# HGRN scores with the queries stationary: four 32-query blocks in four column quarters, one masked copy, a transpose back

## The chip, the cores and the metric

The kernel runs on one core of one Trainium2 chip. The metric is device time in microseconds of one execution of the whole block, median over runs.

## The reference, cut to what matters

A decoder block: 16 meta tokens and 1024 tokens of width 1024 go through an S5 branch and an HGRN2 branch, which are merged, projected and followed by a gated MLP. The change touches the intra-chunk part of the HGRN2 branch, for 8 heads of 128 channels:

```python
def hgrn2_mixer(q, f_logit, i_in, og, lb, norm_g):
    ...
    cum = jnp.cumsum(heads(log_f), axis=3)
    q_in = qh * jnp.exp(cum)
    k_in = kh * jnp.exp(-cum)
    ...
    def chunk_step(state, xs):
        qi, ki, ko, v, dec = xs
        scores = jnp.where(causal, jnp.einsum('bhtd,bhsd->bhts', qi, ki), 0.0)
        o = jnp.einsum('bhts,bhsv->bhtv', scores, v) + jnp.einsum('bhtd,bhdv->bhtv', qi, state)
        state = dec[..., None] * state + jnp.einsum('bhsd,bhsv->bhdv', ko, v)
        return state, o
```

All data are float32.

## The kernel before

The work runs in three stretches. First the projections of the input (`proj_tile`, L166: weights `wh`, `wl` stationary, 24 matmuls of 342 columns to a tile `pj`). From about 195 us to 880 us the loop over heads `h` follows: `main_steps` projects head `h` and some gates (`ga`), one tile per step, while the generators in `fill` advance head `h - 1` (`hgrn_mix`, two halves of 512 tokens) and two S5 halves (`s5_half`); the tables `MIX0`, `MIX1`, `S5A`, `S5B` say at which step each generator is advanced. In the last round (`h` = 8) there is no head left to project, only gates. Then come the output projections, beginning with `whgrn` (`bh`, `bl_`, L935 and after), and the MLP.

The program is not executed in the order written: a scheduler puts the instructions of each engine into a fixed order at build time, and the pools `pj` (3 banks of PSUM), `sm` (5 banks) and the SBUF tags limit how far it may run ahead. On the chip each engine, and SP's DMA queue, works through its own list in that order.

A half of `hgrn_mix` handles 4 chunks of 128 tokens. Each chunk's scores are made in 4 blocks of 32 queries, each against all the keys up to the end of the block: with the keys `Kb` stationary (32, 64, 96 or 128 columns) and 32 queries of `Qb` moving (L726), so scores land with keys on the partitions. Four masked copies, one for each 32 partitions (`copy_predicated`, L734), put them into `sT`, whose never written entries are zero. One step later `sT` is the stationary operand of the output matmuls (L742), next to the state term (L743); `o_norm`, a transpose back (L628) and a gating (`gt`) follow. After the second half `yb_d[h]` is written to DRAM (L748). A float32 matmul shows as two passes in the trace, each a weight load and a matmul; a transpose shows as one.

After the last head, SP loads `mc` from `ga_d` and `yr` from `yb_d` (L932, L934), ACT casts `yr` into `bh`, and the `whgrn` projections begin.

Of the kernel before, what the change touches and what calls it, by code (L numbers as in the profile page):

```python
# [15 lines left out]
ALU = mybir.AluOpType  # L16
# [4 lines left out]
P = 128  # L21
# [30 lines left out]
def block_kernel(  # L52
# [5 lines left out]
    V, S, G, PE, SY = nc.vector, nc.scalar, nc.gpsimd, nc.tensor, nc.sync  # L58
# [19 lines left out]
    def bc(ap, ax, shape):  # L78
        return ap.unsqueeze(ax).to_broadcast(shape)
# [6 lines left out]
    def cst(shape, name, dt=F32):  # L86
        return const.tile(shape, dt, name=name)
# [4 lines left out]
    def sm():  # L92
        return psums[-1].tile([P, 512], F32, tag="sm", name="sm", bufs=1 if len(psums) == 1 else 5)
# [3 lines left out]
    ident = cst([P, P], "ident")  # L97
# [104 lines left out]
    cmask = s5c.tile([P, P], U8, name="cmask")  # L202
# [10 lines left out]
    def masks():  # L213
        for m, starts in ((mV, [(0, 32)]), (mC, []), (mE, [(31, 32)])):
            G.memset(m, 0.0)
            for a, st in starts:
                G.memset(m[:, 0:512].rearrange("p (a b) -> p a b", b=st)[:, :, a : a + 1], 1.0)
        G.memset(mV[:, 512:513], 1.0)
        G.memset(mV[:, 16:528].rearrange("p (a b) -> p a b", b=128)[:, :, 0:1], 1.0)
        G.memset(mC[:, 0:1], 1.0)  # L220
        G.memset(mC[:, 16:528].rearrange("p (a b) -> p a b", b=128)[:, :, 0:1], 1.0)
        G.memset(mE[:, 16:528].rearrange("p (a b) -> p a b", b=128)[:, :, 127:128], 1.0)
        G.memset(mE[:, 15:16], 1.0)
        cmf = p1.tile([P, P], F32, name="cmf")
        G.memset(cmf, 1.0)
        for r in range(4):
            R = slice(32 * r, 32 * r + 32)
            G.affine_select(
                out=cmf[R, 0:32], in_=cmf[R, 0:32], pattern=[[1, 32]], compare_op=ALU.is_ge, fill=0.0, base=0,
                channel_multiplier=-1,  # L230
            )
        V.tensor_copy(out=cmask, in_=cmf)

    def small_consts():
# [245 lines left out]

    consts = small_consts()
    masks()
    for k in range(NK):
        for i, (raw, hi, lo) in enumerate(w01):
# [10 lines left out]
    for k in range(NK):  # L495
# [5 lines left out]
        for s, l in x_cols(k):  # L501
            e = slice(s, s + l)
# [73 lines left out]
    def half(name):  # L576
        return hps[1].tile([P, HB], F32, tag="hh", name=name, bufs=NHH)
# [30 lines left out]
    def chunks(ap):  # L608
        return ap.rearrange("p (n b) -> p n b", n=4)
# [24 lines left out]
    def hgrn_mix(h, hh, carry, q, f, vT, gt):  # L634
        if True:
# [16 lines left out]
            W4 = Wp[:, 16:528].rearrange("p (a b) -> p a b", b=32)  # L652
            Rt, Qb, ko = half("R"), half("Qb"), half("ko")
            R4 = Rt[:, 0:512].rearrange("p (a b) -> p a b", b=32)
# [11 lines left out]
            for i in (1, 2, 3):  # L666
                w = 32 * i - 16
# [37 lines left out]
            for n in range(nn):  # L705
                PE.matmul(  # L706
                    pp[:, n * P : (n + 1) * P], kot[:, n * P : (n + 1) * P], vtok[:, n * P : (n + 1) * P], start=True,
                    stop=True,
# [12 lines left out]
            psc = sm()  # L721
            for n in range(4):
                for i in range(4):
                    e = 16 + KN * n + 128 * i
                    m = 32 * (i + 1)
                    PE.matmul(  # L726
                        psc[:m, n * P + 32 * i : n * P + 32 * i + 32], Kb[:, e : e + m],
                        Qb[:, n * P + 32 * i : n * P + 32 * i + 32], start=True, stop=True,
                    )
            sT = sTs[hh]  # L730
            for r in range(4):
                R = slice(32 * r, 32 * r + 32)
                w = P - 32 * r
                V.copy_predicated(  # L734
                    out=sT[R, :, 32 * r : P], mask=bc(cmask[R, 0:w], 1, [32, 4, w]),
                    data=psc[R, :].rearrange("p (n b) -> p n b", n=4)[:, :, 32 * r : P],
                )
            yield
            po = sm()
            for n in range(4):  # L740
# [9 lines left out]
    def s5_half(hb):  # L750
# [107 lines left out]
        out=m16, in_=m16, pattern=[[1, 2]], compare_op=ALU.is_ge, fill=0.0, base=T0, channel_multiplier=-1  # L858
# [18 lines left out]
            yield from hgrn_proj_in(h, st)  # L877
        yield from gate_steps(NGATE[h])

    MIX0 = {0: 1, 1: 1, 2: 1, 3: 1, 5: 1, 6: 1}  # L880
    MIX1 = {4: 1, 5: 1, 7: 1, 8: 1, 10: 1, 11: 1}
    S5A = {0: 1, 2: 1, 3: 1, 4: 1, 5: 1, 6: 1}
    S5B = {8: 1, 9: 1, 10: 1, 11: 1, 12: 1, 13: 1}
    prev = []
# [13 lines left out]
    Kb = hp.tile([P, 16 + 4 * KN], F32, name="Kb")  # L898
    sTs = [hp.tile([P, 4, P], F32, name=f"sT{i}") for i in range(2)]
    KTs = [sp.tile([P, 4, P], F32, name=f"KT{i}") for i in range(1)]  # L900
    for t in sTs + KTs:
        G.memset(t, 0.0)
    for h in range(1, NK + 1):
        st = []
        carry = hp.tile([P, P], F32, tag="carry", name="carry", bufs=2)
        fill = [
            (hgrn_mix(h - 1, 0, carry, *prev), MIX0), (hgrn_mix(h - 1, 1, carry, *prev), MIX1),
            (s5_half(2 * h - 2), S5A), (s5_half(2 * h - 1), S5B),
        ]
        for u, _ in enumerate(main_steps(h, st)):  # L910
            for g, when in fill:
                step(g, when.get(u, 0))
        for g, _ in fill:
            step(g, 99)
        prev = st
# [74 lines left out]
    for m in range(NK):  # L990
# [15 lines left out]
        for a in range(2):  # L1006
            pt_ = sm()
            for i in range(4):
# [3 lines left out]
                out=ht[:, 4 * a : 4 * a + 4, m * P : (m + 1) * P], in_=pt_.rearrange("p (n b) -> p n b", n=4)  # L1012
# [190 lines left out]
```

## Time and profile before

| | |
|---|---|
| median of 3 runs | 2039.78 us (2030.02 to 2045.96) |
| profiled execution: its own time | 2034.58 us |
| span of its trace | 2032.9 us |
| PE busy | 1982.1 us (98%) |
| DVE busy | 1259.6 us (62%) |
| ACT busy | 563.9 us (28%) |
| mean granted TensorE clock | 0.982 of full speed |

PE is the matmul engine, PEld its weight loads, DVE the vector engine, ACT the scalar engine, SPq the queue from which SP issues DMAs. Since matmuls are pipelined, the recorded durations of neighbours overlap: what a matmul costs is the distance from its start to the next one's. [...]

### The profile page before, as it was taken

To read this page: it belongs to the slowest core of one execution; us is meant where nothing else is said; L and a number is where in the kernel's file an instruction comes from. 1 tells how busy PE (TensorE), PEld (TensorE's weight loads), DVE (VectorE), ACT (ScalarE), POOL (GpSimd) and SP (SyncE) were. 2 spreads that over 40 slices of the span, in tenths; PEclk is the share of its full clock that TensorE was granted. 3 is DMA by queue.
4 is the path that set the end of the run, shared out by engine and by line. 5 is a ranking of instruction groups with operands and counts; after the bars stand their busy time and mean duration, and the time that the engine had idled before them with its cause. 6 is when DMAs were issued, how large, how long until landed. Compare 5 with 4: busy or idle time off the path is not lost.

```text
span 2032.9 us, 30294 instructions
## 1 busy us (share of the span) xinstructions
PE 1982.1 (98%) x12353; PEld 1903.1 (94%) x12353; DVE 1259.6 (62%) x2344; ACT 563.9 (28%) x900; POOL 106.1 (5%) x79
## 2 busy tenths in 40 slices
PE   8999999999999999959999999999999999999997
PEld 7999999999999999959999999999999999999996
DVE  7997767778677687745244533555465555555567
ACT  5422332323223232233122223322222222222224
POOL 3000000000000000000000211000000000000001
PEclk9999999999999999979999999999999999999999
DMA  4216343443434334373223222211111111101102
GB/s 157 99 68 219 95 112 82 109 104 101 107 87 113 88 107 137 112 255 104 63 93 115 83 83 74 95 42 42 52 52 46 39 52 52 53 32 52 52 12 83
DMA packets 100346, 179.20 MB, mean 88 GB/s; under 512 B 28272, under 2 KB 61296, under 8 KB 99440
## 3 DMA queue, kind: packets, MB, share of 16 engines
q1 hardware_dynamic: 100208, 177.28, 28.8%
q8 instruction: 97, 1.59, 0.3%
q14 instruction: 41, 0.34, 0.1%
HBM read 134.41 MB, written 31.94 MB: 82 GB/s over the span
## 4 chain that ended last, share of the span: by engine, by line
PE 83%; DVE 6%; DMA 5%; SPq 1%; ACT 1%; issue 1%; DVEq 0%; ACTq 0%
PE pj L166 63%; PE sm L1100 11%; PE sm L726 3%; DMA Bv<-in_bj_dram 2%; PE sm L796 1%; PE sm L845 1%; PE sm L706 1%; PE sm L743 1%; PE sm L742 1%; PE sm L814 1%; DMA t_d<-tS 1%; DMA yr<-yb_d 1%; DVE wl L61 1%; PE sm L844 0%; DMA wr<-in_wi_dram 0%
## 5 line engine op out<-in xcount | busy, mean ns | idle before, releaser
L166 PE MATMUL pj<-ah,wh 128*128 128x342 f32 (+2 forms) x1632 | 527.0, 323 | 0.2 <-ACT ut L460 0.2
L166 PE MATMUL pj<-al,wh 128*128 128x342 f32 (+2 forms) x1632 | 526.3, 323 | 0.0
L166 PE MATMUL pj<-ah,wl 128*128 128x342 f32 (+2 forms) x1632 | 525.5, 322 | 0.0
L166 PE MATMUL pj<-bh,wh 128*128 128x342 f32 x1440 | 459.2, 321 | 16.5 <-ACT bh L935 14.6
L166 PE MATMUL pj<-bl__9284,wh 128*128 128x342 f32 x1440 | 463.8, 322 | 0.6 <-DVE bl__9284 L61 0.5
L166 PE MATMUL pj<-bh,wl 128*128 128x342 f32 x1440 | 462.8, 321 | 0.0
L166 PEld LDWEIGHTS pj<-ah,wh 128*128 128x128 f32 x1632 | 309.2, 190 | 1.9 <-issue 1.2
L166 PEld LDWEIGHTS pj<-al,wh 128*128 128x128 f32 x1632 | 309.7, 190 | 1.0 <-issue 1.0
L166 PEld LDWEIGHTS pj<-ah,wl 128*128 128x128 f32 x1632 | 309.3, 190 | 0.1
L156 ACT CAST wh<-wr 128x1024 fp32r<-128x1024 f32 x128 | 134.6, 1052 | 619.4 <-PE pj L166 519.6
L166 PEld LDWEIGHTS pj<-bh,wh 128*128 128x128 f32 x1440 | 273.6, 191 | 19.0 <-ACT bh L935 15.5
L166 PEld LDWEIGHTS pj<-bl__9284,wh 128*128 128x128 f32 x1440 | 272.5, 189 | 3.8 <-DVE bl__9284 L61 2.1
L166 PEld LDWEIGHTS pj<-bh,wl 128*128 128x128 f32 x1440 | 272.7, 189 | 1.3
L61 DVE TENSOR_TENSOR wl<-wr,wh 128x1024 fp32r<-128x1024 f32 (+1 forms) x138 | 180.6, 1309 | 113.7 <-ACT wh L156 102.0
L61 DVE TENSOR_TENSOR pre<-pj,rs 128x342 f32<-128x342 f32 x129 | 66.2, 513 | 195.8 <-PE pj L166 195.4
L61 DVE TENSOR_TENSOR ht<-ht,sm 128x512 f32<-128x512 f32 x168 | 110.5, 684 | 65.9 <-PE sm L1100 65.9
L1100 PE MATMUL sm<-dl,xh 128*128 128x512 f32 x336 | 131.3, 391 | 0.0
L1100 PE MATMUL sm<-dh,xh 128*128 128x512 f32 x336 | 130.9, 389 | 0.0
L1100 PE MATMUL sm<-dh,xl 128*128 128x512 f32 x336 | 126.7, 391 | 0.0
L70 DVE SCALAR_TENSOR_TENSOR u<-pre,cws,u 128x1024 f32<-128x1024 f32 (+1 forms) x90 | 113.4, 1260 | 4.9 <-ACT u L73 3.6
L61 POOL TENSOR_TENSOR u<-u 128x1024 f32<-128x1024 f32 x20 | 48.0, 2402 | 624.7 <-DVE u L70 624.7
L1100 PEld LDWEIGHTS sm<-dh,xl 128*128 128x128 f32 x336 | 63.1, 188 | 13.3
(300 smaller groups left out, 2185.6 us busy)
## 6 DMA issues: line engine op xcount, KB each, us to landing
wr<-in_wi_dram SPq DMA_DIRECT2D x54, 512.0 KB
wr<-in_wup_dram SPq DMA_DIRECT2D x44, 512.0 KB
dr<-in_wdn_dram SPq DMA_DIRECT2D x22, 512.0 KB
yr<-y_d SPq DMA_DIRECT2D x16, 516.0 KB
ga_d<-ga SPq DMA_DIRECT2D x48, 171.0 KB
u_d<-ut SPq DMA_DIRECT2D x8, 520.0 KB
t_d<-tS SPq DMA_DIRECT2D x4, 1040.0 KB
Ct<-t_d SPq DMA_DIRECT2D x32, 130.0 KB
```

The costliest lines, as they stand in the source:

```text
L61: e.tensor_tensor(out=o, in0=a, in1=b, op=op)
L70: e.scalar_tensor_tensor(out=o, in0=a, scalar=s, in1=b, op0=op0, op1=op1)
L156: S.copy(out=hi, in_=raw)
L166: PE.matmul(ps[:, :l], w[:, k, :], x[:, k, off + s : off + s + l], start=(n == 0), stop=(n == 3 * NK - 1))
L706: PE.matmul(pp[:, n * P : (n + 1) * P], kot[:, n * P : (n + 1) * P], vtok[:, n * P : (n + 1) * P], start=True, stop=True,)
L726: PE.matmul(psc[:m, n * P + 32 * i : n * P + 32 * i + 32], Kb[:, e : e + m], Qb[:, n * P + 32 * i : n * P + 32 * i + 32], start=True, stop ...
L742: PE.matmul(po[:, c], sT[:, n, :], vtok[:, c], start=True, stop=False)
L743: PE.matmul(po[:, c], Cp[:, 16 + n * P : 16 + (n + 1) * P], St[:, c], start=False, stop=True)
L796: PE.matmul(pk[:16, g * P : (g + 1) * P], bl[:, 0, g, :], Vk[:, g, 0:8, :].rearrange("p k h -> p (k h)"), start=True, stop=True,)
L814: PE.matmul(pw_[:, (g - 2 * a) * NC : (g - 2 * a + 1) * NC], W[:, g].rearrange("p r x -> p (r x)"), U[:, g, :], start=True, stop=True,)
L845: PE.matmul(o, Vk[:, g, 1:9, :].rearrange("p k h -> p (k h)"), w[:, g, 0 : NC - 1], start=False, stop=True)
L1100: PE.matmul(ps, a[:, i * P : (i + 1) * P], w[:, c], start=(j == 0 and n == 0), stop=(j == 1 and n == 2))
```

## The change

The scores are formed with the operands exchanged: for each block the 32 queries are stationary and 128 keys move, so scores land with queries on the partitions, block `i` on partitions `32 i` to `32 i + 31`, which is the matmul's column position in the array. One masked copy over 128x512 replaces the four. A step of its own is added, in which PE transposes the four 128x128 chunks (4 transposes) and ACT copies the result into the buffer `R` (`Rt`), which takes the place of `sT` in the output matmuls. `MIX0` gets a step at 4 and `MIX1` one at 9. `cmask` is built by one `affine_select` in place of four, and `Kb` (2576 columns) is set to zero once, as `sT` and `KT` are.

```diff
-        for r in range(4):
-            R = slice(32 * r, 32 * r + 32)
-            G.affine_select(
-                out=cmf[R, 0:32], in_=cmf[R, 0:32], pattern=[[1, 32]], compare_op=ALU.is_ge, fill=0.0, base=0,
-                channel_multiplier=-1,
-            )
+        G.affine_select(
+            out=cmf, in_=cmf, pattern=[[-1, P]], compare_op=ALU.is_ge, fill=0.0, base=0, channel_multiplier=1
+        )
...
             for n in range(4):
                 for i in range(4):
                     e = 16 + KN * n + 128 * i
-                    m = 32 * (i + 1)
+                    q0 = n * P + 32 * i
                     PE.matmul(
-                        psc[:m, n * P + 32 * i : n * P + 32 * i + 32], Kb[:, e : e + m],
-                        Qb[:, n * P + 32 * i : n * P + 32 * i + 32], start=True, stop=True,
+                        psc[32 * i : 32 * i + 32, n * P : (n + 1) * P], Qb[:, q0 : q0 + 32], Kb[:, e : e + P],
+                        start=True, stop=True,
                     )
-            sT = sTs[hh]
-            for r in range(4):
-                R = slice(32 * r, 32 * r + 32)
-                w = P - 32 * r
-                V.copy_predicated(
-                    out=sT[R, :, 32 * r : P], mask=bc(cmask[R, 0:w], 1, [32, 4, w]),
-                    data=psc[R, :].rearrange("p (n b) -> p n b", n=4)[:, :, 32 * r : P],
-                )
+            sS = sTs[hh]
+            V.copy_predicated(out=sS, mask=bc(cmask, 1, [P, 4, P]), data=chunks(psc))
+            yield
+            pT = sm()
+            for n in range(4):
+                PE.transpose(pT[:, n * P : (n + 1) * P], sS[:, n, :], ident)
+            sT = Rt[:, 0:512].rearrange("p (n b) -> p n b", n=4)
+            S.copy(out=sT, in_=chunks(pT))
             yield
...
-    MIX0 = {0: 1, 1: 1, 2: 1, 3: 1, 5: 1, 6: 1}
-    MIX1 = {4: 1, 5: 1, 7: 1, 8: 1, 10: 1, 11: 1}
+    MIX0 = {0: 1, 1: 1, 2: 1, 3: 1, 4: 1, 5: 1, 6: 1}
+    MIX1 = {4: 1, 5: 1, 7: 1, 8: 1, 9: 1, 10: 1, 11: 1}
...
-    for t in sTs + KTs:
+    for t in [Kb] + sTs + KTs:
         G.memset(t, 0.0)
```

The scheduler's order changes with it. On PE, at the second half of the first head, the program before has the state matmuls (L706), the sixteen score matmuls, four narrow S5 matmuls (L796) and the projections:

```order
L706 MATMUL sm<-vtok,kot 128x128 x3
L726 MATMUL sm<-Qb,Kb 32x32
L726 MATMUL sm<-Qb,Kb 64x32
L726 MATMUL sm<-Qb,Kb 96x32
L726 MATMUL sm<-Qb,Kb 128x32
L726 MATMUL sm<-Qb,Kb 32x32
L726 MATMUL sm<-Qb,Kb 64x32
L726 MATMUL sm<-Qb,Kb 96x32
L726 MATMUL sm<-Qb,Kb 128x32
```

The changed program has at the same place the scores as sixteen equal matmuls:

```order
L703 MATMUL sm<-vtok,kot 128x128 x3
L723 MATMUL sm<-Kb,Qb 32x128 x16
L166 MATMUL pj<-al,wh 128x342
L166 MATMUL pj<-ah,wl 128x342
L166 MATMUL pj<-ah,wh 128x342
```

and 24 projection matmuls after them the transposes, ahead of the narrow S5 matmuls:

```order
L166 MATMUL pj<-ah,wl 128x342
L166 MATMUL pj<-ah,wh 128x342
L732 MATMUL sm<-ident,sT_2046 128x128 x4
L793 MATMUL sm<-Vk,bl 16x128 x4
L166 MATMUL pj<-al,wh 128x342
L166 MATMUL pj<-ah,wl 128x342
```

So the mask has 24 projection matmuls of PE's list to be copied in, and the narrow S5 matmuls moved behind the transposes.

In the last round, before, PE's list goes from the first half's scores over S5 (L814) and the value transposes (L646) to projections, 22 matmuls of them until the output matmuls, and 195 from this block of scores to the last S5 matmul:

```order
L726 MATMUL sm<-Qb,Kb 128x32
L814 MATMUL sm<-U,W 128x130 x4
L646 MATMUL sm<-ident,vT 128x128 x4
L166 MATMUL pj<-ah,wh 128x342
L166 MATMUL pj<-al,wh 128x342
L166 MATMUL pj<-ah,wl 128x342
```

In the changed program no projection is left there; from the scores to the last S5 matmul nothing but HGRN and S5 work stands in the list:

```order
L625 MATMUL sm<-ident,on 128x2
L723 MATMUL sm<-Kb,Qb 32x128 x16
L811 MATMUL sm<-U,W 128x130 x4
L732 MATMUL sm<-ident,sT_2045 128x128 x4
L643 MATMUL sm<-ident,vT 128x128 x4
L739 MATMUL sm<-vtok,R 128x128
L740 MATMUL sm<-St,C 128x128
```

The 195 projection matmuls stand earlier in PE's list: round by round HGRN and S5 work has moved back behind projections.

On SP, at the end of this stretch, the program before has the last swap of the S5 scan (`ws<-x`), the write of `yb_d` of the last head, the writes of `y_d`, and then the loads for the `whgrn` projections:

```order
L823 DMA ws<-x 64x520
L865 DMA ga_d_122<-ga 128x342
L147 DMA wr<-in_whgrn_dram 128x1024
L748 DMA yb_d_106<-gt 128x1026
L853 DMA y_d_98<-yo 8x16x129 x4
L932 DMA mc<-ga_d_115 128x1026
L934 DMA yr<-yb_d_99 128x1026
```

In the changed program `yb_d` is written ahead of the swap, and the loads stand ahead of `y_d`:

```order
L745 DMA yb_d_106<-gt 128x1026
L819 DMA ws<-x 64x520
L820 DMA ws<-x 64x520
L929 DMA mc<-ga_d_115 128x1026
L931 DMA yr<-yb_d_99 128x1026
```

Ten of the sixteen loads now come ahead of the write of `y_d`. The first load of `mc` waits for the write of `yb_d` in both programs.

## Rows read from the trace of the kernel before

**Rows 1.** The page: busy time of the engines, and the chain by engine.

```profile
PE 1982.1 (98%) x12353; PEld 1903.1 (94%) x12353; DVE 1259.6 (62%) x2344; ACT 563.9 (28%) x900; POOL 106.1 (5%) x79
...
PE 83%; DVE 6%; DMA 5%; SPq 1%; ACT 1%; issue 1%; DVEq 0%; ACTq 0%
```

**Rows 2.** Timeline of PE around one block of scores: start us, us, engine, line.

```profile
258.79 3.74 PE L726 MATMUL sm<-Qb,Kb 128*32 128x32 f32 x32
262.46 1.05 PE L796 MATMUL sm<-Vk,bl 128*16 128x128 f32 x8
```

**Rows 3.** Line L726 over the whole span: duration ns min/median/max, first and last start.

```profile
L726 PE MATMUL sm<-Qb,Kb x512: 196/249/403, 226.4 to 856.9; 128*32 128x32 f32 x43, 128*64 128x32 f32 x43, 128*128 128x32 f32 x43, 128*96 128x32 f32 x42
```

**Rows 4.** Timeline of PE: narrow matmuls with 128 moving columns; four transposes.

```profile
216.37 0.83 PE L796 MATMUL sm<-Vk,bl 128*16 128x128 f32 x6
...
195.80 0.60 PE L646 MATMUL sm<-ident,vT 128*128 128x128 f32 x4
```

**Rows 5.** Eight us after blocks of scores: width, busy by engine, PEclk, DMA.

```profile
230.00:238.00 8.00, 8.00 (x51) 8.00 (x51) 7.84 (x19) 1.78 (x4) 0.10 (x1) 0.79 0.16 35
262.00:270.00 8.00, 8.00 (x61) 7.67 (x61) 3.07 (x9) 1.42 (x5) 0.00 (x0) 1.00 0.21 44
...
517.00:525.00 8.00, 8.00 (x37) 7.03 (x37) 3.21 (x10) 1.82 (x3) 0.00 (x0) 0.57 0.16 35
```

**Rows 6.** Timeline of PE: projections after a block of scores, at both clocks.

```profile
233.45 0.49 PE L166 MATMUL pj<-ah,wh 128*128 128x342 f32 x1
233.73 0.49 PE L166 MATMUL pj<-al,wh 128*128 128x342 f32 x1
...
234.40 0.32 PE L166 MATMUL pj<-al,wh 128*128 128x342 f32 x1
234.55 0.32 PE L166 MATMUL pj<-ah,wl 128*128 128x342 f32 x1
```

**Rows 7.** The last round as one window, from its first scores to PE's end.

```profile
823.50:879.90 56.40, 52.20 (x369) 50.26 (x369) 38.33 (x91) 13.52 (x38) 0.00 (x0) 0.96 0.45 125
```

**Rows 8.** Timeline of DVE in the last round.

```profile
827.33 2.10 DVE L734 COPY_PREDICATED sT<-cmask,sm 32x512 f32<-32x512 uint8 x4 [0.29 <-PE sm L726]
...
840.79 1.22 DVE L61 TENSOR_TENSOR wl<-wr,wh 128x1024 fp32r<-128x1024 f32 x1
...
849.73 0.22 DVE L715 COPY St<-carry 128x128 f32<-128x128 f32 x1
853.31 1.23 DVE L61 TENSOR_TENSOR wl<-wr,wh 128x1024 fp32r<-128x1024 f32 x1 [3.36 <-ACT wh L156]
...
857.20 1.31 DVE L734 COPY_PREDICATED sT<-cmask,sm 32x512 f32<-32x512 uint8 x2 [1.64 <-PE sm L726]
...
860.02 0.21 DVE L61 TENSOR_TENSOR kt<-kt,di 16x64 f32<-16x64 f32 x1
```

**Rows 9.** Timeline at the end of the last round: SP's queue, then ACT and PE.

```profile
860.26 5.65 SPq L807 DMA_DIRECT2D KT<-kt  x8
...
873.10 0.55 SPq L823 DMA_DIRECT2D ws<-x  x1
...
875.80 0.32 SPq L748 DMA_DIRECT2D yb_d<-gt  x1
...
882.28 0.33 SPq L932 DMA_DIRECT2D mc<-ga_d  x1
...
890.20 1.22 PE L166 MATMUL pj<-bh,wh 128*128 128x342 f32 x3 [10.08 <-ACT bh L935]
...
907.67 1.05 ACT L935 CAST bh<-yr 128x1026 fp32r<-128x1026 f32 x1 [0.20 <-DMA yr<-yb_d]
```

**Rows 10.** The chain that ended last, in order of time, between the two stretches.

```profile
875.80 6.41 DMA yb_d<-gt
```

**Rows 11.** Prices of the added steps: an ACT copy, POOL's zeroing of 512 columns.

```profile
809.85 0.59 ACT L687 COPY kot<-sm 128x512 f32<-128x512 f32 x1 [0.40 <-PE sm L685]
...
L902 POOL MEMSET sT<- x2: 525/526/527, 200.1 to 200.6; 128x512 f32 x2
```

## The prediction

> **What bounds the kernel now.** I read the page first, for the busiest engine and the chain [rows 1]: PE is busy 98% of the span and carries 83% of the chain that ended last, DVE and DMA some 5% each. A microsecond taken from PE's list counts, then, wherever PE has work queued, and one given to ACT or DVE costs nothing there. The exception is the seam at the end of the last round, where PE runs dry and a chain of DVE work and DMAs sets the time [rows 7 to 10].
>
> Then the timeline around one block of scores [rows 2]: it starts at 258.79 and the next line at 262.46, so a block holds PE for 3.67 us, with 32 passes (16 matmuls in two passes each). Line L726 has 512 passes [rows 3], 16 blocks.
>
> Last the granted clock behind the blocks. Of the sixteen stretches of 8 us that begin near a block's end, seven have a clock under 1.00: five at 0.79 like the first of [rows 5], two at 0.57 like the last, and nine at 1.00. I saw none behind other float32 work in the rounds. All seven follow blocks of scores whose rows move 32 columns at a time.
>
> **The change, part by part.**
>
> *Scores.* Removed per block: 3.67 us. Added: 32 passes of 32 stationary and 128 moving columns. The nearest row is the narrow S5 matmul, 16 stationary and 128 moving columns: six passes in 0.83 us, of which the last one's own length is about 0.27, so 0.56 us for five distances, 0.11 us a pass [rows 4]. That row always uses the same quarter of the array. If the quarters don't work at the same time, 32 passes cost 3.5 us. If they do: the two passes of one matmul use the same quarter and must follow each other, but the second pass of a block can run beside the first pass of the next, which is in another quarter. That makes 17 distances for 16 matmuls, 1.9 us. If all four quarters were always full, a quarter of 3.5, 0.9 us. The trace has no two neighbours in different quarters, so both ends stay; I take 1.9, since separate weights and separate output partitions leave nothing that the pair would share except the stream of passes in PE's list. To it come 0.2 us for entering and leaving the narrow layout (the blocks of before paid some of that already).
>
> [...]
>
> *Transposes.* Four transposes: 0.60 us less the last one's 0.27 is 0.33 for three distances, so 4 x 0.11 = 0.44 us of PE per block [rows 4]. The copy to SBUF, 0.59 us [rows 11], lies on ACT, which is 28% busy [rows 1].
>
> Per block, 3.67 - 1.9 - 0.2 - 0.44 = 1.1 us saved. This counts in the 14 blocks of the first seven rounds, where projections follow: **-16 us**. (Without overlap: 3.67 - 3.5 - 0.2 - 0.44 = -0.5, so +7 us; with all quarters full, 2.1 x 14, so -30.)
>
> *The clock.* Five stretches lose 0.21 and two lose 0.43 of full speed over 8 us. [...] The new blocks are half as long and move 128 columns in each pass, as the S5 matmuls do that are followed by no lower clock. I take the whole of it: **-14 us**, with 0 as the other end.
>
> *DVE and POOL.* One masked copy of 128x512 instead of four: the four take 2.1 us, the largest of them some 0.7 [rows 8], so 1.4 us less of DVE per block, which in the rounds is idle time anyway. Zeroing `Kb` takes five times the 0.53 us of a 512 column memset [rows 11], 2.7 us of POOL at the start of the rounds, while PE projects; DVE's first write of `Kb` may wait 1.5 us, covered by projections. One `affine_select` for four at the start: nothing.
>
> *New waits in the rounds.* PE's transposes wait for DVE's mask, PE's output matmuls for ACT's copy. The order puts 17 to 25 projection matmuls (2.7 to 3.9 us) ahead of each, against 0.7 us of DVE and 0.6 of ACT with perhaps a cast of 1.05 us in front, as long as the one of [rows 9]. Nothing, then, in my sum; if a queue is late, PE stands still with all projections behind it.
>
> *The last round.* This is the loss. The 195 projection matmuls that stood between its first scores and PE's end are gone from there, done earlier: 195 x 0.157 = 30.6 us that come ahead. In return the stretch from 823.5 on gets shorter, and the question is by how much. Before, it takes 56.4 us to PE's end, with DVE busy 38.3 [rows 7], and DVE works through almost without a pause until 849.95 [rows 8]. To `kt` at 860.0 it is 36.5 us. What falls away there: two splits of projection weights that are then long done (2.4 us), the wait for the cast in front of one (3.4), the shorter masks (2 x 1.4) and a shorter block of scores (1.6): 10.2 us. What comes new: the second half's transposes, and the narrow S5 matmuls behind them, with `kt`'s copy, some 2 us. So `kt` comes 8 us earlier, after 28. From there the same DMAs: eight writes of `KT`, 5.65 us of issue, swaps, scan [rows 9]. But `yb_d`, whose landing of 6.4 us the loads of `mc` wait for [rows 10], now goes out ahead of the last swap, 4 us sooner. The loads can then start 12 us sooner than at 882.28, which is what the seam hangs on: from `mc` to the last cast of `bh` at 908.7 it is 26 us of transfers [rows 9, 10]. The projections start free of it 12 us earlier in this stretch's own time, so the net loss is 30.6 - 12 = 18.6; as a few loads are taken out of the crowd behind `y_d`, I take **+17 us**. [...]
>
> **Sum.** -16 - 14 + 17 = -13, on the profiled execution's own 2034.6: **2021 us**. Against the median of 2039.8 that is 0.9% less. The profiled execution is 5 us under the median; I leave that out, since the lower clock behind the scores is probably much of the spread, and it is what should go.
>
> **Rivals.**
>
> *The quarters take turns.* Every pass costs 0.11 us as in [rows 4]. For it: that is the only price of a narrow pass in the trace. Against: the passes there all hit one quarter. Price: +7 for 14 blocks, +2 in the last round, with +17 and the clock's -14: 2047, slower than before's 2034.6. It decides from about 3.1 us a block on, where the whole change breaks even.
>
> *All four quarters full.* -30 instead of -16: 2007. Against: the two passes of a matmul follow each other in PE's list.
>
> *The clock falls as before.* The transposes and passes that fill only a part of the array could be too little for it. For it: seven of sixteen stretches now. Then the 14 us stay: 2035, no change.
>
> *The new links hold PE up in the rounds.* The two waits per block go to engines that work in order. At 1 us for each of 14 blocks and half of that at the second link, 21 us: 2042. Against: 2.7 us of cover at each.
>
> **How the numbers follow.** Forecast 0.5, quarters take turns 0.2, all full 0.08, clock as before 0.12, links 0.1. The forecast's own range is its last round, 2010 to 2035. For 8 in 10 I reach from 2000, half the way into the third case, to 2050, past the second. A difference of 1% (20 us) is about what a measurement of this kernel can tell. Faster by more than that is under 2019.4: 0.4 of the forecast, most of the third case, little of the others: 0.34. Slower by more is over 2060: a part of the second and of the links, 0.11. The rest 0.55.
>
> **What would show it.** Starts of scores to the next line 2.1 us apart (3.7 for turns, 1.1 for all full). Stretches of 8 us behind the scores at clock 1.00. Four transposes in 0.6 us, and no idle time of PE in front of them. In the last round PE idle for 20 us or more between its scores and S5's end, and the loads of `mc` ahead of `y_d`. I would be wrong altogether if PE waits for weights in the earlier rounds, because projections have moved ahead of SP's loads there; no row shows that.

## The result, and the profile after

| | before | after |
|---|---|---|
| median | 2041.01 us (4 runs, 2030.02 to 2045.96) | 2014.88 us (4 runs, 2013.91 to 2015.77) |
| ratio to before | | 0.988, 95% interval 0.986 to 0.991 |
| profiled execution | 2034.58 us, span 2032.9 | 2014.2 us, span 2012.3 |

The change makes the kernel 1.2% faster. The page of the profile after has PE less busy and a chain that is PE's for a little more of the span than before [rows 1]:

```profile
PE 1939.7 (96%) x12417; PEld 1867.0 (93%) x12417; DVE 1239.1 (62%) x2296; ACT 571.1 (28%) x916; POOL 108.1 (5%) x77
...
PE 86%; DVE 4%; DMA 3%; SPq 1%; issue 1%; ACT 1%; DVEq 0%; ACTq 0%
```

**The scores.** Timeline of PE around the first block, answering to [rows 2]:

```profile
226.09 1.08 PE L723 MATMUL sm<-Kb,Qb 128*32 128x128 f32 x32
227.10 1.16 PE L811 MATMUL sm<-U,W 128*128 128x130 f32 x8
...
230.95 0.60 PE L732 MATMUL sm<-ident,sT 128*128 128x128 f32 x4
231.39 0.60 PE L643 MATMUL sm<-ident,vT 128*128 128x128 f32 x4
```

From start to next start a block takes 1.01 us (3.67 before), and so do all fifteen blocks that are followed by other work. The four transposes take 0.44. How 32 passes fit into 1.01 us is seen in a window over the first 60 ns of the next block, which starts at 254.96, for this line alone (PE busy with the number of passes, then PEld with that of weight loads):

```profile
254.90:255.02 0.12, 0.06 (x4) 0.06 (x8) 1.00 0.66 251
```

Four passes and eight weight loads begin in these 60 ns, where passes in one quarter stand 0.11 us apart [rows 4]: all four quarters run.

**The clock.** Eight us behind the blocks, fourteen windows (one like these is [rows 5]). All fourteen have 1.00, three of them here. The last row is another place: PE stood idle there for 3.19 us, up to 706.56, and the granted clock was 0.50 from 705.54 to 712.35:

```profile
228.00:236.00 8.00, 8.00 (x59) 7.98 (x58) 7.26 (x18) 3.53 (x7) 0.10 (x1) 1.00 0.35 104
257.00:265.00 8.00, 8.00 (x57) 7.53 (x56) 1.50 (x6) 2.49 (x4) 0.00 (x0) 1.00 0.19 52
504.00:512.00 8.00, 8.00 (x55) 7.53 (x53) 2.81 (x7) 3.02 (x5) 0.00 (x0) 1.00 0.29 86
...
703.00:711.00 8.00, 4.81 (x19) 4.53 (x17) 6.84 (x12) 2.98 (x7) 0.00 (x0) 0.66 0.21 69
```

**Waits in the rounds.** PE's waits from the first scores to the last round (total us, times, longest):

```profile
PE pj L166 <- ACT gt L595: 3.2, 1, 3.2
PE sm L842 <- DVE w L61: 1.9, 2, 1.1
PE sm L682 <- DVE ko L61: 0.9, 1, 0.9
PE sm L625 <- DVE on L61: 0.5, 1, 0.5
```

Neither the transposes' wait for the mask nor the output matmuls' wait for the copy is in it. The first line is new. ACT's timeline shows what it waited for:

```profile
706.06 0.79 ACT L595 COPY gt<-pj 128x342 f32<-128x342 f32 x2 [7.03 <-DMA yb_d<-gt]
```

`gt` of head `h` lies in the buffer that head `h - 2` used, and cannot be filled until that head's `yb_d` has been written.

**The last round.** It starts at 812.35 in place of 823.50 [rows 7]. One window over it up to S5's end, then PE's timeline at its idle times:

```profile
812.30:860.00 47.70, 21.32 (x182) 18.72 (x182) 32.97 (x82) 9.17 (x30) 0.00 (x0) 0.74 0.40 114
```

```profile
812.35 1.08 PE L723 MATMUL sm<-Kb,Qb 128*32 128x128 f32 x32
...
829.80 1.09 PE L625 MATMUL sm<-ident,on 128*128 128x128 f32 x4 [10.46 <-DVE on L61]
...
839.11 0.66 PE L732 MATMUL sm<-ident,sT 128*128 128x128 f32 x4 [1.62 <-DVE sT L728]
...
857.29 0.80 PE L842 MATMUL sm<-w,Vk 128*128 128x129 f32 x2 [7.26 <-DVE w L61]
...
875.00 0.65 PE L166 MATMUL pj<-bl__9330,wh 128*128 128x342 f32 x1 [12.04 <-DVE bl__9330 L61]
...
892.62 0.42 PE L166 MATMUL pj<-bh,wh 128*128 128x342 f32 x1 [4.42 <-DVE al L61]
```

PE is busy 21.3 of 47.7 us, at a mean clock of 0.74 (52.2 of 56.4 and 0.96 before). `kt` on DVE, the row that answers to the last of [rows 8]:

```profile
841.38 0.21 DVE L61 TENSOR_TENSOR kt<-kt,di 16x64 f32<-16x64 f32 x1 [2.33 <-ACT kt L798]
```

SP's queue and ACT at the seam, answering to [rows 9]:

```profile
849.87 0.32 SPq L745 DMA_DIRECT2D yb_d<-gt  x1
...
854.43 0.33 SPq L929 DMA_DIRECT2D mc<-ga_d  x1
...
883.95 1.06 ACT L932 CAST bh<-yr 128x1026 fp32r<-128x1026 f32 x1 [0.21 <-DMA yr<-yb_d]
```

**Where the time went.** Up to the last round's first scores the changed kernel is 11.2 us ahead (812.35 against 823.50), with 195 projection matmuls more behind it, worth 30.6: 41.8 us gained. From there to the end of the span it needs 1200.0 us against 1209.4, 9.4 less although 30.6 us of work are gone: 21.2 lost. Together 20.6, the difference of the spans.

### The profile page after: what moved, and what is told of

The parts are those of the page before. It is cut to its first block, busy times and chain, and to the rows that moved or that the text cites. A ratio compares the mean times of both kernels' runs of the same rounds, so it can differ in the third digit from the quotient of the medians.

```text
span 2012.3 us, 30381 instructions
## 1 busy us (share of the span) xinstructions
PE 1939.7 (96%) x12417; PEld 1867.0 (93%) x12417; DVE 1239.1 (62%) x2296; ACT 571.1 (28%) x916; POOL 108.1 (5%) x77
## 4 chain that ended last, share of the span: by engine, by line
PE 86%; DVE 4%; DMA 3%; SPq 1%; issue 1%; ACT 1%; DVEq 0%; ACTq 0%
PE pj L166 68%; PE sm L1097 11%; DMA Bv<-in_bj_dram 1%; DMA yr<-yb_d 1%; DMA yb_d<-gt 1%; PE sm L793 1%; SPq L804 1%; PE sm L723 1%; PE sm L703 1%; PE sm L811 1%; PE sm L842 1%; PE sm L739 1%; PE sm L740 1%; PE sm L841 1%; DVE ht L61 0%
## 5 line engine op out<-in xcount | busy, mean ns | idle before, releaser
L166 PEld LDWEIGHTS pj<-bl__9330,wh 128*128 128x128 f32 x1440 | 272.3, 189 | 14.2 <-DVE bl__9330 L61 12.5
L1097 PEld LDWEIGHTS sm<-dh,xl 128*128 128x128 f32 x336 | 63.0, 188 | 13.3
```

The costliest lines, as they stand in the source:

```text
L166: PE.matmul(ps[:, :l], w[:, k, :], x[:, k, off + s : off + s + l], start=(n == 0), stop=(n == 3 * NK - 1))
L1097: PE.matmul(ps, a[:, i * P : (i + 1) * P], w[:, c], start=(j == 0 and n == 0), stop=(j == 1 and n == 2))
```

## The experiments

Two things had to be told apart. First, what made the block 1.01 us long and the clock stay up. Second, what emptied the last round. My theory A: not the work of the transposes, but the link that they add to a head's chain (score, mask, transpose, copy, output), by which the order written at build time sets each head later beside the projections. Rivals: the work itself (D), the scores or masks or a last round bound by DVE whatever stands in PE's list (B), and a chain that no longer fits into a round (C).

| run | median us | ratio to before | 95% interval |
|---|---|---|---|
| the changed kernel | 2014.88 | 0.988 | 0.986 to 0.991 |
| two_quarters | 2021.27 | 0.992 | 0.990 to 0.995 |
| quarter_by_quarter | 2036.52 | 0.998 | 0.996 to 1.000 |
| qbq_twice | 2093.06 | 1.027 | 1.025 to 1.030 |
| no_transposes | 1975.96 | 0.967 | 0.964 to 0.971 |
| off_chain | 1977.3 | 0.971 | 0.968 to 0.973 |
| before_plus_transposes | 2102.65 | 1.030 | 1.027 to 1.033 |
| gates_10 | 2068.89 | 1.013 | 1.010 to 1.016 |
| gates_11 | 2069.38 | 1.013 | 1.010 to 1.016 |
| tables_later | 1983.3 | 0.973 | 0.971 to 0.976 |
| tables_later2 | 1992.21 | 0.978 | 0.975 to 0.980 |
| tables_gate_1 | 1981.43 | 0.972 | 0.971 to 0.974 |
| tables_gate_0 | 1983.64 | 0.974 | 0.972 to 0.976 |

### The quarters

```diff
-            for n in range(4):
-                for i in range(4):
+            for i in range(4):
+                for n in range(4):
```

> The changed kernel with the two loops around the score matmuls exchanged, i outside and n inside: four neighbours in PE's list use the same quarter before the next quarter comes. Same work, same order otherwise. Theory O (passes run beside each other only when neighbours in the list are in different quarters): 32 passes of 0.11 us less three seams, a block of 3.3 us in place of 1.01, 14 x 2.3 + 2 = 34 us: 2049 us if the granted clock stays at 1.00 behind the blocks, some 14 us more, 2063, if it falls behind them as it did before the change. Theory L (PE looks ahead in its list past a busy quarter): 1.0 us a block and 2015. The clock: if its fall came from 3.6 us of a block with little in it, it comes back here, at 0.6 to 0.8 over the next 8 us behind several blocks; if it came from rows of 32 moving columns, it stays at 1.00.

Timeline of PE at one block, then three windows in that block, for this line alone (the counts are of passes and loads in work):

```profile
257.79 2.46 PE L723 MATMUL sm<-Kb,Qb 128*32 128x128 f32 x32
260.18 0.42 PE L166 MATMUL pj<-al,wh 128*128 128x342 f32 x1
```

```profile
257.78:257.90 0.12, 0.11 (x1) 0.11 (x2) 1.00 1.02 376
...
258.24:258.25 0.01, 0.01 (x2) 0.01 (x1) 1.00 0.00 0
258.26:258.27 0.01, 0.01 (x4) 0.01 (x2) 1.00 0.00 0
```

One pass begins where four did, and the block takes 2.39 us: order matters, so theory L falls, but 2.39 is not 3.3 either, so O falls in its strict form. The last two windows show why. The first quarter's passes begin 0.109 us apart; at 258.25 its fifth begins, and within 20 ns a second pass with it, which must be one of the next quarter. In the list three passes of the first quarter, not yet begun, stand ahead of that one. An estimate from these starts fits: if each next quarter begins four distances after the one ahead of it, as if about four passes of a quarter were kept waiting, three times four and eight are 20 distances of 0.109, 2.2 us, and the first and last are longer (0.13 and 0.20). What in PE brings this about, no trace shows. The time follows the block: 15 times 1.38 is 20.7 us, and 21.6 were measured. The clock is 1.00 behind all fourteen blocks. The next two runs put the estimate to the test:

```diff
-            for n in range(4):
-                for i in range(4):
+            for n, i in [(n, 2 * a + j) for a in range(2) for n in range(4) for j in range(2)]:
```

> The changed kernel with its score matmuls in another order: first the blocks of quarters 0 and 1 of all four chunks, in turn, then those of quarters 2 and 3. By the reading of quarter_by_quarter (a next quarter begins when some four passes of the quarter ahead of it are still to go, as if each quarter could keep four passes waiting): eight passes in each quarter, the second pair begins four passes after the first, twelve distances of 0.109 and the first of 0.13, 1.35 us a block, and 14 x 0.35 + 1 = 6 us more than the changed kernel, 2021. If a quarter kept nothing waiting beyond its next pass: sixteen distances, 1.8 us, 2027. If order didn't matter: 1.01 and 2015.

```profile
255.10 1.54 PE L723 MATMUL sm<-Kb,Qb 128*32 128x128 f32 x32
256.57 0.42 PE L166 MATMUL pj<-al,wh 128*128 128x342 f32 x1
```

1.47 us a block, nearest to the 1.35 of four waiting passes and away from 1.8 and 1.01. If the second pair of quarters begins right behind the fifth passes of the first pair, with three in each still to begin, the distances above (0.13, 0.109, 0.20) make 1.44 us by estimate.

```diff
-                    PE.matmul(
+                    for _ in range(2):
+                        PE.matmul(
```

> As quarter_by_quarter, each score matmul issued twice, with the same result. By the same reading: sixteen passes a quarter, the next quarter begins twelve passes later, 3 x 12 + 16 = 52 distances of 0.109, 5.7 us a block; in time 16 x 3.3 = 53 us more than quarter_by_quarter, 2089. The clock: a block longer than those of the kernel before (3.6 to 4.1 us), of passes of 32 stationary and 128 moving columns. If the fall of the clock behind blocks came from their length with little in them, it is back, behind at least seven blocks, and 14 us or more come on top. If it came from 32 moving columns, the clock stays at 1.00 behind all of them.

```profile
259.66 5.96 PE L724 MATMUL sm<-Kb,Qb 128*32 128x128 f32 x64
265.55 0.42 PE L166 MATMUL pj<-al,wh 128*128 128x342 f32 x1
```

```profile
266.00:274.00 8.00, 8.00 (x55) 7.53 (x55) 1.46 (x6) 1.91 (x4) 0.00 (x0) 1.00 0.15 43
```

5.88 us against the 5.7 expected; if the next quarter begins right behind the thirteenth of sixteen passes, again with three still to begin, the same distances make 5.84. The window behind this block has the clock at 1.00, and so have all fourteen such windows. Blocks of 5.88 us, more than half as long again as the 3.6 to 4.1 of before, were followed by no lower clock here; the seven falls of before all stood at blocks whose rows move 32 columns. Those blocks also had 32 to 128 stationary columns; that was not tried by itself.

### What emptied the last round

```diff
-            pT = sm()
-            for n in range(4):
-                PE.transpose(pT[:, n * P : (n + 1) * P], sS[:, n, :], ident)
-            sT = Rt[:, 0:512].rearrange("p (n b) -> p n b", n=4)
-            S.copy(out=sT, in_=chunks(pT))
-            yield
+            sT = sS
```

> The changed kernel with the four transposes, ACT's copy and the added step left out: the masked scores go to the output matmuls as they lie, so the attention is formed from untransposed scores. Scores, mask and everything else as changed. In the list of PE the last round has its projections again: 216 stand between its first scores and the end of S5 (195 before the change, none after it). Theory A (the loss at the end comes from the longer chain of a head, score, mask, transpose, copy, output, which moved the projections out of the last round): the 14 blocks of transposes fall away, 6 us, and the last round gets back the 21 us that it lost: 2015 - 6 - 21 = 1988 us, range 1980 to 1995. Theory B (the loss comes from the new scores or the longer mask, or the last round is bound by DVE and DMAs whatever stands in PE's list): only the 6 us: 2009. A block of scores 1.0 us in both.

With them the tables lose their added steps: `MIX0` and `MIX1` are as before the change.

The last round starts at 771.66 with 216 projections left, and PE waits first at the seam:

```profile
831.83 1.22 PE L166 MATMUL pj<-bh,wh 128*128 128x342 f32 x3 [11.69 <-ACT bh L927]
```

1976 us, 39 under the changed kernel: theory A's direction, but 12 us more than its 27, and below its range. The last round gives back 31 rather than 21 (from its first scores to the span's end 1203 us with 216 projections, 34 us, against 1200.0 with none), because it is filled better than it was before the change. Of the rest, 6 are the transposes and some 3 the low clock at the wait for `gt` (0.50 for 6.8 us in the changed kernel); the waits themselves are no fewer, 7.9 us in these rounds against 6.5. B falls.

The counterpart, transposes and copy put into the kernel before:

```diff
             yield
+            pT = sm()
+            for n in range(4):
+                PE.transpose(pT[:, n * P : (n + 1) * P], sT[:, n, :], ident)
+            sT = Rt[:, 0:512].rearrange("p (n b) -> p n b", n=4)
+            S.copy(out=sT, in_=chunks(pT))
+            yield
             po = sm()
```

> The kernel before, with its own scores and its four masks, and the added step alone: four transposes and ACT's copy between mask and output matmuls, so the output is formed from scores transposed once too often. PE's list has no projection in the last round, as in the changed kernel. Theory A: 14 x 0.44 = 6 us of transposes and 21 us lost in the last round: 2041 + 27 = 2068 us, range 2060 to 2075; blocks of scores stay at 3.6 to 4.1 us and the granted clock falls behind about seven of them. Theory B: 2047. If the transposes alone had ended the low clock behind the scores, 14 us less than either.

The tables get the added steps of the changed kernel. 2103, 35 more than theory A expected and outside its range, and 56 more than B. PE's waits from its first scores to the last round:

```profile
PE pj L166 <- ACT gt L598: 19.4, 3, 12.0
PE sm L851 <- DVE w L61: 3.5, 3, 2.7
PE sm L628 <- DVE on L61: 3.0, 2, 1.9
```

What I had left out is the first line, the wait for `gt`'s buffer: heads that fall behind write `yb_d` later, and the next head but one then holds up PE. The last round costs 30 us here (1209.0 us to the end of the span, as before, with 195 projections less). PE's waits in the rounds, 27 us against 7 before, and these 9 us more are 29 of the 35; the rest was not worked out, and the clock is low behind the longest wait too: behind its 11.95 us projections stand 0.28 to 0.29 us apart from 678.05 to 683.18, and 0.16 after that. The clock is under 1.00 in nine of fourteen windows behind the blocks, so the transposes are not what ended its falls.

Work and link are told apart by making the transposes for nobody:

```diff
-                PE.matmul(po[:, c], sT[:, n, :], vtok[:, c], start=True, stop=False)
+                PE.matmul(po[:, c], sS[:, n, :], vtok[:, c], start=True, stop=False)
```

> The changed kernel with one edit: the output matmuls read the masked scores as they lie (so the attention is formed from untransposed scores), while transposes and copy are all still made, with nobody waiting for them. PE, ACT and DVE do the same work as in the changed kernel; only the link in a head's chain is gone. PE's list has 259 projections behind the first scores of the last round. Theory A (the link in the chain costs, not the work of the transposes): as the run without transposes, 1976, and the 6 us of PE for them: 1982 us, range 1976 to 1990. Theory D (the work itself costs, on PE, on ACT or by the buffers that it holds): as the changed kernel, 2010 to 2015.

All work is done, and the time is 1977. In its rounds PE waits once, 0.4 us:

```profile
PE sm L732 <- DVE sT L728: 0.4, 1, 0.4
```

D falls: the 37.6 us between this and the changed kernel are the link. With the wait the edit also frees `R` at the copy instead of at the output matmuls; the two were not told apart, though `C` and `vtok` of the same half, from the same rotation of buffers, are held until those matmuls in every variant. The 6 us of the transposes don't show beside no_transposes, since PE waits 0.4 us in these rounds and 7.9 in those. Without its waits, PE is 0.5 us longer in them here although 43 projections (6.8 us) more are left for the last round, so the added work does cost PE some 7 us.

### Giving the last round its work back

```diff
-NGATE = (3, 1, 1, 1, 1, 1, 1, 1, 6)
+NGATE = (3, 0, 0, 0, 0, 1, 1, 1, 10)
```

> The changed kernel with four of the gates' projections moved from rounds 1 to 4 to the last round, NGATE = (3, 0, 0, 0, 0, 1, 1, 1, 10); nothing else. 289 projection matmuls stand between the first scores of the last round and the end of S5, 158 between its second scores and there. Theory A: the idle time of PE in the last round (35 us of the 48 from its first scores to the end of S5) is filled with them, the 21 us come back, and a part of the 10 us that the kernel before already lost: 1990 us, range 1983 to 1996. Rival C: rounds 1 to 4, shorter by 11 us each, can no longer cover the chain of one head (DVE is busy 60 us of 81 in a round), and PE waits there: 2010 or more, with idle time of PE over 2 us at transposes, output matmuls or narrow S5 matmuls of these rounds.

> As the run with ten gates in the last round, but eleven, NGATE = (3, 0, 0, 0, 0, 0, 1, 1, 11). 375 projection matmuls stand behind the first scores of the last round, 121 of them behind the last S5 matmul, beside the transfers from which the output projections are fed. Theory A: the last round and the seam are both covered, 15 us more than with ten gates: 1975 us, range 1968 to 1988. Rival C: five rounds without cover, PE waits in them: as slow as ten gates or slower, above 1990.

Both are 54 us slower than the changed kernel. PE's waits in the rounds of gates_10:

```profile
PE pj L166 <- ACT gt L595: 35.5, 5, 11.6
PE sm L625 <- DVE on L61: 30.1, 7, 8.5
```

Rival C, and dearer than I had put it: 66 us of waits, at `gt`'s buffer and the transposes of `on` rather than at the places that it named. Work can't be moved to the end by taking it from the rounds, which need it as cover.

The other way is to leave the work and change the order:

```diff
-    MIX0 = {0: 1, 1: 1, 2: 1, 3: 1, 4: 1, 5: 1, 6: 1}
-    MIX1 = {4: 1, 5: 1, 7: 1, 8: 1, 9: 1, 10: 1, 11: 1}
+    MIX0 = {0: 1, 1: 1, 2: 1, 3: 1, 5: 1, 6: 1, 8: 1}
+    MIX1 = {4: 1, 5: 1, 7: 1, 8: 1, 10: 1, 11: 1, 13: 1}
```

> The changed kernel with other steps for the halves of a head: MIX0 = {0, 1, 2, 3, 5, 6, 8}, MIX1 = {4, 5, 7, 8, 10, 11, 13}, so transposes one step after they stand now, and the output's gating two. Nothing else. In PE's list the heads keep their distance to the projections, 360 projections from one head's scores to the next one's as in the run without transposes, and 238 stand behind the first scores of the last round (none in the changed kernel). Theory A: the last round is covered again, as in the run without transposes, with 6 us more on PE: 1984 us, range 1976 to 1998. Rival C (a head's chain as lengthened doesn't fit a round, whatever the order; the list then waits): PE stands idle in the rounds and the time is over 2010.

1983 us, as theory A had it. PE's waits in the rounds, then the first one in the last round:

```profile
PE sm L842 <- DVE w L61: 4.4, 6, 1.0
PE sm L682 <- DVE ko L61: 0.3, 1, 0.3
```

```profile
838.22 1.22 PE L166 MATMUL pj<-bh,wh 128*128 128x342 f32 x3 [13.25 <-ACT bh L932]
```

The link is in place and its work too, and the loss is gone, the wait for `gt` as well. So the chain does fit into a round; what cost was where the list put it. The transposes and the gating stand later in the tables, and the heads come earlier in the list. This version beats both kernels: 0.973 of before.

In tables_later2 the transposes stay at their steps:

```diff
-    MIX0 = {0: 1, 1: 1, 2: 1, 3: 1, 4: 1, 5: 1, 6: 1}
-    MIX1 = {4: 1, 5: 1, 7: 1, 8: 1, 9: 1, 10: 1, 11: 1}
+    MIX0 = {0: 1, 1: 1, 2: 1, 3: 1, 4: 1, 6: 1, 8: 1}
+    MIX1 = {4: 1, 5: 1, 7: 1, 8: 1, 9: 1, 11: 1, 13: 1}
```

> As tables_later, with the transposes left at their steps 4 and 9 and only the output matmuls and the gating later: MIX0 = {0, 1, 2, 3, 4, 6, 8}, MIX1 = {4, 5, 7, 8, 9, 11, 13}. 284 projections stand behind the first scores of the last round, 60 of them behind the last S5 matmul, beside the transfers of the seam. Theory A: 1980 us, range 1972 to 1998. Rival C: over 2010.

1992, inside the range and 9 us behind tables_later, though more work is left for the last round. A wait of 3.3 us for `on` in the rounds is part of it, and PE's wait at the seam is longer, 16.9 us against 13.3.

Last, tables_later with one gate moved to the last round, for its 13 us at the seam:

```diff
-NGATE = (3, 1, 1, 1, 1, 1, 1, 1, 6)
+NGATE = (3, 0, 1, 1, 1, 1, 1, 1, 7)
```

> tables_later with one gate moved from round 1 to the last round, NGATE = (3, 0, 1, 1, 1, 1, 1, 1, 7). 93 projections stand behind the last S5 matmul, beside the transfers of the seam (21 in tables_later, where PE then stood idle 13.6, 2.2 and 4.2 us). Theory A: 72 projections of 0.157, 11 us, are taken out of the idle time of the seam: 1972 us, range 1968 to 1980. Rival C: round 1, shorter by 11 us, makes PE wait in it or behind it, or the last gates' writes hold up the loads of mc: 1983 or more.

```diff
-NGATE = (3, 1, 1, 1, 1, 1, 1, 1, 6)
+NGATE = (2, 1, 1, 1, 1, 1, 1, 1, 7)
```

> As tables_gate_1, but the gate is taken from the projections ahead of the rounds, where no head runs beside them, NGATE = (2, 1, 1, 1, 1, 1, 1, 1, 7). No round gets shorter, the same 93 projections stand at the seam: 1972 us by theory A, range 1968 to 1980; the tables of S5 and the parameters, which are made beside that stage, could need its cover: then 1980 or more, with PE waiting about 150 to 220 us.

Neither differs from tables_later by more than the spread of the runs. Both lie above theory A's range, and 1981 lies under the 1983 of the rival. In tables_gate_1 the seam moves along with the work; its chain shows by what:

```profile
822.93 10.08 DMA mc<-ga_d
...
833.07 7.68 DMA ga_d<-ga
...
840.93 1.05 ACT bh L932
```

The last gates' own writes and the loads of `mc` behind them hold up the first `bh`, and PE waits 11.25 us for it at 842.03. But that is only half of it. From the last round's first scores to the end of the span it takes 1213.4 us against 1208.8 in tables_later, 4.6 more for 11.3 us of work, so some 6.7 us of idle time were filled. The rounds took them back: PE waits 9.3 us in them against 4.7. In tables_gate_0 PE waits 5.6 us between 100 and 226 us, against 1.0. So both halves of the rival came: the cover was missed where the gate had stood, and the writes held up the loads.

## Why the prediction held, and which of its sizes were off

2021 us were forecast with 2000 to 2050 around it, and 2014.88 came. In the profiled executions the difference is 20.4 us against the 13 of the sum. The signs of the three terms were right; two of the sizes were off, one of them by half. That the time lies only 6 us from the forecast is partly luck: the scores gave 15 us more than the sum had, and the last round took 4 back and a wait that the sum lacked some 3. The range of 50 us covers the forecast's mechanism and its rival alike.

**Scores, -16.** Mis-sized: 14 x (3.67 - 1.01 - 0.44) = 31. The step of the sum that failed is "the two passes of one matmul use the same quarter and must follow each other, but the second pass of a block can run beside the first pass of the next". PE did not take its list one neighbour at a time: in quarter_by_quarter the next quarter's first pass began, at 258.25, while three passes ahead of it in the list had not, and with the same lead the blocks of two_quarters and qbq_twice would be 1.44 and 5.84 us by estimate; they took 1.47 and 5.88. In the changed kernel each quarter has only two passes to wait before another chunk comes, and four passes began in the first 60 ns of a block. So the mechanism was that of the rival "All four quarters full", whose time of 2007 failed because the last round took more back. "The quarters take turns" would have been right only with another order of the loops.

**The clock, -14.** All seven falls are gone. One came new, at the wait for `gt`'s buffer: 6.8 us at 0.50 (705.54 to 712.35). No row of before gives the 14 itself. Its trace has the seven falls at 0.50 throughout, 30.6 us in all, five of 3.4 us and two of 6.8; one of each:

```profile
230.75:234.15 3.40, 3.40 (x16) 3.40 (x15) 3.33 (x9) 1.75 (x4) 0.10 (x1) 0.50 0.33 72
...
517.47:524.28 6.81, 6.81 (x28) 5.92 (x27) 3.04 (x9) 1.10 (x2) 0.00 (x0) 0.50 0.17 38
```

Projections stand 0.28 to 0.29 us apart in such a stretch and 0.15 to 0.16 at 1.00 [rows 6], so by estimate 14 us of the 30.6 were lost, and 3 of the new 6.8. This size was right as far as the balance can tell: 31 and 14, less these 3, make 42, and 41.8 were gained ahead of the last round. PE's waits in the rounds are about equal, 6.9 us before and 6.5 after. The reason given for it was half right. The new blocks move 128 columns, as the longer ones of qbq_twice do; that they are short does not decide it, since its 5.88 us are followed by 1.00 too. Whether it is the 32 moving columns or the changing width of the stationary operand stays open.

**DVE, POOL and new waits, 0.** The mask takes 0.7 us as costed, and neither of the two waits appears in the rounds. A wait came that no step had: the 3.2 us for `gt`'s buffer, small here, 19 to 36 us where heads fall further behind.

**The last round, +17.** 21.2 were lost. The chain went as worked out: `kt` on DVE at 841.38, 29.0 us after the first scores (28 forecast), the last cast of `bh` over at 885.01, 72.7 us after them where it was 85.2, 12.5 us sooner (12 forecast). That leaves 30.6 - 12.5 = 18.1. The remaining 3 lie behind that cast, where the sum ended: PE waits 4.42 us there at 892.62, against 1.08 at the same place before. The loads of `mc` start 16.7 us sooner in this stretch's own time, but that does not come through to the casts. The ends of the forecast's own range, 2010 and 2035, were the author's estimate; this term came as 21.2, with a mean clock of 0.74 from the first scores to S5's end.

What the prediction took as given, that the list had emptied the last round, has its cause shown now: the link of transposes and copy (before_plus_transposes, off_chain), through the order and not through its own length on the chip (tables_later). How the order comes to set a head later for a longer chain is inside the scheduler and was not tried, so this part stays open.

**Rivals.** "The clock falls as before" and "the new links hold PE up" did not come.

## What to carry to other kernels

When a step is added to a chain that runs beside a bound engine, count in the new list what is left beside the last round, and where a step drifts, try the table of steps before anything else: here that was worth 32 us, more than the change itself. Small matmuls in different column quarters ran beside each other here where the quarters alternate in the list within a few passes: a block took 1.01 us with all four in turn, 1.47 with two, 2.39 quarter by quarter. Work that covers a chain can't be moved to a later place for nothing: look first at what the place it leaves was hiding.

## What the runs showed of the hardware that was not expected

- In the changed kernel four column quarters gave 3.5 times: 32 float32 passes of 32 stationary and 128 moving columns took 1.01 us (254.96 to 255.97), where in the trace of before passes in one quarter stand 0.109 us apart, which makes 3.5 for 32. In quarter_by_quarter the same passes took 2.39 us, in two_quarters 1.47.
- In quarter_by_quarter passes did not start in the order of the list. Its 32 passes, of which eight in a row share a quarter, took 2.39 us (257.79 to 260.18), less than the 3.3 that theory O allows, and the next quarter's first pass began within 20 ns of 258.25, while three passes ahead of it in the list had not. So PE did not work through its list strictly in order there, as it is said of every engine where the kernel before is described.
- In before the passes of 32 moving columns saved nothing on average: 3.67 us for 32 [rows 2], 0.115 each, beside 0.109 for a pass of 128 moving columns. But they are not alike. From the first to the second pass of a matmul it is 0.05 us with 32 stationary columns, 0.08 with 64 and 0.11 with 96 or 128; from the last pass of a chunk to the next chunk's first, where 128 stationary columns give way to 32, it is 0.21 (medians over the sixteen blocks of before).
- It is at these blocks that the granted clock of before fell in the rounds, seven times of sixteen, to 0.50 for 3.4 or 6.8 us, from 1.15 us ahead of a block's end to 0.75 us behind it; five of the seven blocks have a mean clock of 0.86 to 0.97 themselves. PE was busy without a pause in all of them.
